# A two-layer decoder trunk: sums of the feed-forward layer on another engine, its second norm a quad later, and the last norm laid out as columns

## The chip, the cores and the metric

One core of a Trainium2 chip runs the kernel. The metric is the device time of one execution in microseconds; the kernel is run several times and the median is given, and one execution is recorded by the hardware profiler. TensorE (PE) multiplies matrices, VectorE (DVE) and ScalarE (ACT) work on tiles of 128 partitions, GpSimd (POOL) does so too, and SyncE (SP) issues most of the DMAs. PSUM holds what TensorE accumulates, SBUF everything else.

## The reference

Only the parts that the change touches are shown in full.

```python
def rmsnorm(x, g):
    xf = x.astype(jnp.float32)
    y = xf * lax.rsqrt(jnp.mean(xf * xf, axis=-1, keepdims=True) + EPS)
    return (y * g.astype(jnp.float32)).astype(x.dtype)

def swiglu(h, w_in, w_out):
    a = h @ w_in
    gate, up = jnp.split(a, 2, axis=-1)
    return (jax.nn.silu(gate) * up) @ w_out

def reference(x, mem, mix_norm, ...):
    for i in range(DEPTH):                       # DEPTH = 2
        h = rmsnorm(x, mix_norm[i])
        ...                                      # layer 0: HGRN2, layer 1: gMLP; and memory attention
        x = x + heads @ w_out[i]
        x = x + swiglu(rmsnorm(x, ffn_norm[i]), w_ffn_in[i], w_ffn_out[i])
    return rmsnorm(x, final_norm)
```

`x` is 1 x 1024 x 1024 (tokens by features), the feed-forward layer has 2816 hidden features, everything is float32.

## The kernel before

Activations lie with the features on the partitions: a tile is 128 features by 512 tokens, a "half" of the sequence, and `xn[half][kb]` is the residual stream, 8 tiles to a half. Every float32 product is made of three matmuls of a reduced type: an operand is cast to a high part (`hi` or `wh`, a cast on ScalarE, L150 and L130), the rest is the low part (`lo` or `wl`, a subtraction on VectorE, L152 and L132), and L457 (in the feed-forward layer; L157 to L159 and L684 elsewhere) multiplies hi by hi, hi by lo and lo by hi.

`ffn_in` takes the first product of the feed-forward layer in "quads": a quad is a 2 x 2 block of weight tiles against a 2 x 2 block of activations, done with seven products, named "1" to "7", in place of eight. So sums and differences of weights and of activations have to be made first. Three quads are opened early, while the output projection still runs, and the first two (`early`) go through all seven products side by side. The order is: `head1` (product "1") of the three quads, `head2` (product "2"), then products 3, 5, 6, 7 and 4 of the early two. `ready_b` makes the operands of the coming product out of the normed activations of the second half, which need `r`, the second norm's factor: `rest.rstd()` issues its matmul (L210) and then the chain in `rsqrt` (L223 adds eps, L227 and L228 are Ln and Exp, L229 to L231 one Newton step). It is called after the `head1` of quad 0. Ahead of product "6", `early_sums` makes the four weight sums of quad 2 on VectorE (L433 to L436; the third one is the weight of product "6"), and `ready_b("4")` makes the four tiles `t4` on VectorE (L541). L505 adds product "7" of an early quad.

`ffn_out` adds the second product to the residual. In layer 1 its last product ("4", from `CUT` = 4 on) runs in two slices of 256 tokens of the second half; L692 adds a block to the residual, `Sum.add` squares it on ScalarE (L196), and at the end of a slice `rstd` sums over the features: L210 multiplies by a matrix of ones, here in five passes, one for `acc` and one for each of the four newest squares. `final` then scales eight tiles on VectorE (L1178) and SyncE sends them out (L1179).

The tile framework orders each engine's instructions by a schedule of its own, and puts semaphore waits where a tile depends on another; an engine works strictly in its order.

## Time and profile before

| | us |
|---|---|
| median of three runs (lowest, highest) | 2127.53 (2127.23, 2128.64) |
| the profiled execution, its own time | 2128.59 |
| span of its trace | 2126.9 |
| TensorE busy (share) | 2097.6 (99%) |
| VectorE busy (share) | 1376.7 (65%) |
| ScalarE busy (share) | 902.5 (42%) |
| GpSimd busy (share) | 90.5 (4%) |

The span is the time from the first to the last event of the trace; 1.7 us of the execution lie around it. Busy time of TensorE counts matmuls of either clock level alike, so the granted clock has to be read beside it. An instruction's duration in the timeline is longer than the distance to the next one of its engine where the two overlap: matmuls of 128x512 are shown with 0.39 us and follow each other every 0.2265 us (three in 0.68 us). A row "x4" groups four instructions in a row. The value in brackets is the engine's idle time before the instruction and what ended it.

### The profile page before, as it was taken

The page shows a single profiled execution, that of the slowest core. Times are in us where ns is not written, and L with a number is a line of the kernel's source. Part 1 is how long each engine was busy: PE and PEld are TensorE (multiplying, and loading weights), DVE is VectorE, ACT ScalarE, POOL GpSimd, SP SyncE. Part 2 cuts the span into 40 slices and gives each one's busy share as a digit, 9 for nine tenths or more (in the row PEclk, how much of TensorE's full clock was granted, in tenths as well). Part 3 has the DMA queues.
Part 4 walks back from the last instruction along what each step waited for, and adds up shares of the span by engine and source line. Part 5 has one row for each costly group of instructions (what it writes and reads, how often), then busy time and mean ns, then how long its engine had stood idle before and what let it go on. Part 6 is the DMA issues. An engine that isn't in the chain of part 4 may idle for free.

```text
span 2126.9 us, 29399 instructions
## 1 busy us (share of the span) xinstructions
PE 2097.6 (99%) x11414; PEld 1739.3 (82%) x11414; DVE 1376.7 (65%) x2357; ACT 902.5 (42%) x1639; POOL 90.5 (4%) x90
## 2 busy tenths in 40 slices
PE   8999999999999999999999999999999999999998
PEld 7978788788778888888888997787788888888887
DVE  8685665763974655548986744547854554569884
ACT  6444442442543333334454534734433333343462
POOL 1100000001100000000001000011000000000012
PEclk9999999999999999999999999999999999999999
DMA  5400101132022221228454221131122221266442
GB/s 190 121 29 21 31 12 50 31 106 73 20 73 87 85 94 60 90 89 269 152 183 140 95 70 31 45 111 44 40 90 89 84 94 60 87 210 218 132 131 85
DMA packets 84811, 197.84 MB, mean 93 GB/s; under 512 B 9536, under 2 KB 11712, under 8 KB 84672
## 3 DMA queue, kind: packets, MB, share of 16 engines
q1 hardware_dynamic: 84672, 195.97, 28.1%
q8 instruction: 89, 1.46, 0.3%
q14 instruction: 50, 0.41, 0.1%
HBM read 163.95 MB, written 31.98 MB: 92 GB/s over the span
## 4 chain that ended last, share of the span: by engine, by line
PE 88%; DVE 5%; issue 1%; ACT 1%; DVEq 0%; ACTq 0%
PE mm L457 27%; PE mm L684 11%; PE sm L457 10%; PE sm L684 8%; PE mm L157 8%; PE mm L158 8%; PE mm L159 8%; PE sm L945 2%; DVE lo L152 1%; PE sm L357 1%; PE sm L346 1%; PE sm L1025 1%; PE sm L210 1%; PE sm L1006 1%; PE sm L1012 1%
## 5 line engine op out<-in xcount | busy, mean ns | idle before, releaser
L130 ACT CAST wh<-raw 128x512 fp32r<-128x512 f32 x454 | 271.0, 620 | 303.2 <-PE mm L158 106.4
L132 DVE TENSOR_TENSOR wl<-raw,wh 128x512 fp32r<-128x512 f32 x454 | 308.4, 693 | 101.4 <-ACT wh L130 91.8
L457 PE MATMUL mm<-hi,wh 128*128 128x512 f32 x832 | 324.5, 391 | 3.6 <-ACT wh L130 1.8
L457 PE MATMUL mm<-lo,wh 128*128 128x512 f32 x832 | 323.8, 391 | 0.0
L457 PE MATMUL mm<-hi,wl 128*128 128x512 f32 x832 | 323.3, 390 | 0.0
L157 PE MATMUL mm<-hi,wh 128*128 128x512 f32 x640 | 255.3, 399 | 6.2 <-ACT wh L130 6.1
L159 PE MATMUL mm<-hi,wl 128*128 128x512 f32 x640 | 253.4, 396 | 0.0
L158 PE MATMUL mm<-lo,wh 128*128 128x512 f32 x640 | 252.0, 394 | 0.0
L457 PEld LDWEIGHTS mm<-hi,wh 128*128 128x128 f32 x832 | 157.0, 189 | 37.8 <-ACT wh L130 2.7
L457 PEld LDWEIGHTS mm<-hi,wl 128*128 128x128 f32 x832 | 156.9, 189 | 32.8
L457 PEld LDWEIGHTS mm<-lo,wh 128*128 128x128 f32 x832 | 156.9, 189 | 32.7
L505 DVE TENSOR_TENSOR c<-mm,c 128x512 f32<-128x512 f32 x44 | 30.4, 690 | 191.5 <-PE mm L457 188.6
L157 PEld LDWEIGHTS mm<-hi,wh 128*128 128x128 f32 x640 | 120.8, 189 | 34.7 <-ACT wh L130 6.9
L159 PEld LDWEIGHTS mm<-hi,wl 128*128 128x128 f32 x640 | 120.7, 189 | 27.2 <-issue 2.1
L158 PEld LDWEIGHTS mm<-lo,wh 128*128 128x128 f32 x640 | 120.7, 189 | 27.1 <-issue 2.1
L684 PE MATMUL mm<-hi,wh 128*128 128x512 f32 (+1 forms) x380 | 142.9, 376 | 0.0
L684 PE MATMUL mm<-hi,wl 128*128 128x512 f32 (+1 forms) x380 | 141.9, 373 | 0.0
L684 PE MATMUL mm<-lo,wh 128*128 128x512 f32 (+1 forms) x380 | 141.9, 373 | 0.0
L457 PE MATMUL sm<-lo,wh 128*128 128x512 f32 x352 | 136.6, 389 | 0.0
L457 PE MATMUL sm<-hi,wl 128*128 128x512 f32 x352 | 136.6, 389 | 0.0
L457 PE MATMUL sm<-hi,wh 128*128 128x512 f32 x352 | 136.3, 389 | 0.0
L204 POOL TENSOR_TENSOR acc<-acc,sq 128x512 f32<-128x512 f32 x38 | 56.1, 1475 | 1616.6 <-ACT sq L196 1615.7
(263 smaller groups left out, 3955.8 us busy)
## 6 DMA issues: line engine op xcount, KB each, us to landing
raw<-in_wu_dram SPq DMA_DIRECT2D x168, 512.0 KB, 4.1
raw<-in_wu_dram SPq DMA_DIRECT2D x114, 256.0 KB, 3.5
hd<-c SPq DMA_DIRECT2D x88, 256.0 KB, 3.0
hid<-hd SPq DMA_DIRECT2D x88, 256.0 KB, 4.5
s<-in_wu_dram SPq DMA_DIRECT2D x22, 256.0 KB, 4.5
xin<-in_xT_dram SPq DMA_DIRECT2D x16, 256.0 KB, 5.6
xn<-in_xT_dram SPq DMA_DIRECT2D x16, 256.0 KB, 4.9
xs<-xn SPq DMA_DIRECT2D x16, 256.0 KB, 4.6
```

The lines of the kernel that those rows point to most:

```text
L130: nc.scalar.copy(hi, src)
L132: nc.vector.tensor_tensor(lo, src, hi.bitcast(F32), op=ALU.subtract)
L152: nc.vector.tensor_tensor(lo, src, hi.bitcast(F32), op=ALU.subtract)
L157: nc.tensor.matmul(ps, ah, bh, start=first, stop=False)
L158: nc.tensor.matmul(ps, ah, bl, start=False, stop=False)
L159: nc.tensor.matmul(ps, al, bh, start=False, stop=last)
L204: (nc.vector if self.count > 5 else self.adder).tensor_tensor(self.acc, self.acc, sq, op=ALU.add)
L210: nc.tensor.matmul(ps, ones_d, x, start=i == 0, stop=i == len(parts) - 1)
L457: nc.tensor.matmul(ps, a, b, start=start and i == 0 and k == 0, stop=i == 3 and k == 2, skip_group_check=True)
L505: nc.vector.tensor_tensor(self.p, self.b, self.p, op=ALU.add)
L684: nc.tensor.matmul(banks[d][:, sl], a, b, start=start and f == 0 and k == 0, stop=f == FH - 1 and k == 2, skip_group_check=True,)
L945: nc.tensor.matmul(o, keys, qd[:, queries].rearrange("p (b u n) -> p b u n", u=2, n=n)[:, :, 1, :], start=True, stop=True,)
```

## The change

There are four edits.

- In `rsqrt` the addition of eps on VectorE moves behind Ln and Exp in the code (everywhere the function is used). Ln takes eps as its own bias, so both read the same sums.
- In `ffn_in`, in both layers, the four `t4` differences and the four `early_sums` of quad 2 are made by GpSimd in place of VectorE, and `rest.rstd()` comes after the `head1` of quad 1.
- In the last slices (layer 1), three of the four newest squares are added to `acc` on VectorE, so that the matrix of ones is multiplied by two tiles in place of five. For the last slice the new `rstd_last` makes the means as columns (squares as the weights, one column of ones moving), takes the root of 128x2 numbers, spreads them and brings them back into rows with four transposes, twice, into two banks of PSUM; the tables of ScalarE aren't loaded again. Gains of three output tiles (`GAINED`) are multiplied in ahead of time.
- `final` lets GpSimd scale those three tiles and VectorE the other five, and the last slice's eight transfers go out from SyncE and ScalarE in turn.

```diff
+        def rstd_last(self):
+            nt = self.n // P
+            parts = [self.acc] + self.tails
+            ps = sm_ps()[:, :nt]
+            for t in range(nt):
+                for i, x in enumerate(parts):
+                    nc.tensor.matmul(
+                        ps[:, t : t + 1], x[:, t * P : (t + 1) * P], ones_d[:, 0:1],
+                        start=i == 0, stop=i == len(parts) - 1,
+                    )
+            r = rsqrt(ps, None, nt)
+            rb = nrm.tile([P, HALF], F32, name="rb", tag="n")[:, : self.n]
+            nc.vector.tensor_copy(
+                rb.rearrange("p (t f) -> p t f", f=P), r.unsqueeze(2).broadcast_to([P, nt, P])
+            )
+            res = []
+            for _ in range(2):
+                ps = sm_ps()[:, : self.n]
+                for t in range(nt):
+                    nc.tensor.transpose(ps[:, t * P : (t + 1) * P], rb[:, t * P : (t + 1) * P], ident)
+                res.append(ps)
+            return res
...
-            r = Sum(self.adder, sl.stop - sl.start, self.reload)
+            r = Sum(nc.vector, sl.stop - sl.start, self.reload)
...
-        nc.vector.tensor_scalar(a, ps, EPS, None, op0=ALU.add)
         if after is not None:
             with tc.issue_after(after.ins):
                 load_log_tables()
         nc.scalar.activation(r, ps, AF.Ln, bias=eps)
         nc.scalar.activation(r, r, AF.Exp, scale=-0.5)
+        nc.vector.tensor_scalar(a, ps, EPS, None, op0=ALU.add)
...
-        def early_sums(self):
+        def early_sums(self, eng=nc.vector):
-            nc.vector.tensor_tensor(a["22"], a["21"], a["22"], op=ALU.add)
+            eng.tensor_tensor(a["22"], a["21"], a["22"], op=ALU.add)
...
-                    nc.vector.tensor_tensor(d, first[4 + i][0], first[i][0], op=ALU.subtract)
+                    nc.gpsimd.tensor_tensor(d, first[4 + i][0], first[i][0], op=ALU.subtract)
...
             q.head1(t)
-            if i == 0:
+            if i == 1:
                 r = rest.rstd()
...
-                    q.early_sums()
+                    q.early_sums(nc.gpsimd)
...
-        sums = [Sum(), Sum()]
+        sums = [Sum(), Sum(reload=layer == 0)]
...
-                            add("4", d, total, sl, True)
-                        for _ in done(1, total.rstd(), sl):
+                            add("4", d, total, sl, d == 3)
+                        for _ in done(1, total.rstd_last() if sl.start else [total.rstd()] * 2, sl):
...
+            rv, rs = r
+            if sl.start:
+                rs = nrm.tile([P, HALF], F32, name="rs", tag="n")[:, : sl.stop - sl.start]
+                nc.scalar.copy(rs, r[1])
+            for n, d in enumerate((3, 0, 4, 5, 1, 6, 7, 2)):
+                o = xn[half][d][:, sl]
+                if d < GAINED:
+                    nc.gpsimd.tensor_tensor(o, o, rs, op=ALU.mult)
                 else:
+                    nc.vector.scalar_tensor_tensor(o, o, gain(C_FIN + d), rv, op0=ALU.mult, op1=ALU.mult)
+                (nc.scalar if sl.start and n % 2 else nc.sync).dma_start(out=out[d, half, :, sl], in_=o)
```

In the changed kernel the lines have other numbers: L152 is L153, L433 to L436 are L458 to L461, L457 is L482, L500 is L525, L505 is L530, L535 is L560, L541 is L566, L550 and L554 are L575 and L579, L130 is L131.

First place, layer 0, end of the early quads, on VectorE. `raw<-raw` at L433 to L436 are the weight sums, `t` at L541 the four differences, `c` are partial results of products. Before:

```order
L152 TENSOR_TENSOR lo<-hfb,hi 128x512
L434 TENSOR_TENSOR raw<-raw 128x512
L152 TENSOR_TENSOR lo<-hfb,hi 128x512
L435 TENSOR_TENSOR raw<-raw 128x512
L500 TENSOR_TENSOR c_5717<-sm,c_5717 128x512
L436 TENSOR_TENSOR raw<-raw 128x512
L500 TENSOR_TENSOR c_5732<-sm,c_5732 128x512
L541 TENSOR_TENSOR t_5735<-hfa 128x512
L541 TENSOR_TENSOR t_5737<-hfa 128x512
L541 TENSOR_TENSOR t_5739<-hfa 128x512
L541 TENSOR_TENSOR t_5741<-hfa 128x512
L152 TENSOR_TENSOR lo<-t_5735,hi 128x512
```

And GpSimd after the change, in the same place:

```order
L566 TENSOR_TENSOR t_5735<-hfa 128x512
L566 TENSOR_TENSOR t_5737<-hfa 128x512
L458 TENSOR_TENSOR raw<-raw 128x512
L566 TENSOR_TENSOR t_5739<-hfa 128x512
L459 TENSOR_TENSOR raw<-raw 128x512
L566 TENSOR_TENSOR t_5741<-hfa 128x512
L460 TENSOR_TENSOR raw<-raw 128x512
L461 TENSOR_TENSOR raw<-raw 128x512
```

The eight stand in one row on GpSimd, the two kinds in turn; on VectorE they are gone, and the low parts of `t` follow those of `hfb` with only two L525 and one L579 between.

Second place, the same stretch on ScalarE. `wh_5822` is the cast weight of product "6" of quad 2, made of the third weight sum; `hi_5743` to `hi_5755` are the casts of the four `t4`. Before:

```order
L130 CAST wh_5822<-raw_5099 128x512
L130 CAST wh_5826<-raw_5695 128x512
L550 ACTIVATE c12_5717<-c12_5717 128x512
L130 CAST wh_5830<-raw_5695 128x512
L130 CAST wh_5834<-raw_5099 128x512
L150 CAST hi_5743<-t4_5735 128x512
```

After:

```order
L575 ACTIVATE c12_5717<-c12_5717 128x512
L131 CAST wh_5822<-raw_5099 128x512
L151 CAST hi_5743<-t4_5735 128x512
L131 CAST wh_5826<-raw_5695 128x512
L151 CAST hi_5747<-t4_5737 128x512
L131 CAST wh_5830<-raw_5695 128x512
L151 CAST hi_5751<-t4_5739 128x512
```

The cast of the weight now stands directly ahead of the cast of the first `t4`, and the other weight casts stand between those of `t4`. On TensorE two matmuls of product "6" of quad 2 stand ahead of the first of product "4" of quad 0 in both kernels.

Third place, the end of the program, on ScalarE. `xn_12713` and `xn_12900` are the output tiles 0 and 2, which GpSimd scales first and last after the change; `xn_13035` and `xn_13066` are tiles 5 and 6. Before:

```order
L196 ACTIVATE sq_18383<-xn_13066 128x256
L196 ACTIVATE sq_18407<-xn_13097 128x256
L179 ACT_TABLE_LOAD
L227 ACTIVATE r_18415<-sm_18409,eps_84 128x256
L228 ACTIVATE r_18415<-r_18415 128x256
```

After:

```order
L197 ACTIVATE sq_18412<-xn_13097 128x256
L251 ACTIVATE r_18419<-sm_18414,eps_84 128x2
L252 ACTIVATE r_18419<-r_18419 128x2
L1213 COPY rs_18435<-sm_18432 128x256
L1221 DMA out_0_dram<-xn_12713 128x256
L1221 DMA out_0_dram<-xn_12900 128x256
L1221 DMA out_0_dram<-xn_13035 128x256
L1221 DMA out_0_dram<-xn_13066 128x256
```

Behind the root, now on two columns, ScalarE copies the scales and issues four of the eight transfers, that of tile 2 second.

## Rows read from the trace of the kernel before

**Rows 1.** The page, section 1: busy time of TensorE and the others.

```profile
PE 2097.6 (99%) x11414; PEld 1739.3 (82%) x11414; DVE 1376.7 (65%) x2357; ACT 902.5 (42%) x1639; POOL 90.5 (4%) x90
```

**Rows 2.** TensorE's waits: engine, line, releaser, us in total, times, longest.

```profile
PE sm L210 <- DVE acc L204: 3.1, 2, 1.6
PE mm L457 <- ACT wh L130: 1.8, 2, 0.9
PE mm L457 <- DVE c L505: 1.8, 2, 0.9
...
PE mm L157 <- DVE qm L814: 0.9, 1, 0.9
```

**Rows 3.** Timeline: start us, us, engine, line, [idle before]; layer 0's second norm.

```profile
558.36 1.13 PE L210 MATMUL sm<-acc,ones_d 128*128 128x512 f32 x2 [1.54 <-DVE acc L204]
...
560.24 0.69 ACT L227 ACTIVATE r<-sm,eps 128x512 f32<-128x512 f32 x1 [0.77 <-DVE a L223]
```

**Rows 4.** Timeline, TensorE, end of layer 0's early quads.

```profile
594.85 0.39 PE L457 MATMUL mm<-hi,wh 128*128 128x512 f32 x1
...
596.83 0.50 PE L457 MATMUL mm<-hi,wh 128*128 128x512 f32 x1 [0.92 <-ACT wh L130]
...
598.46 0.50 PE L457 MATMUL mm<-hi,wh 128*128 128x512 f32 x1 [0.90 <-DVE c L505]
...
603.13 0.39 PE L457 MATMUL mm<-hi,wh 128*128 128x512 f32 x1
```

**Rows 5.** Timeline, VectorE and ScalarE in the same stretch.

```profile
586.29 1.88 DVE L535 TENSOR_TENSOR hfb<-hfb 128x512 f32<-128x512 f32 x3
...
593.03 1.14 ACT L130 CAST wh<-raw 128x512 fp32r<-128x512 f32 x2 [2.28 <-DVE raw L435]
...
594.72 2.48 DVE L541 TENSOR_TENSOR t<-hfa 128x512 f32<-128x512 f32 x4
```

**Rows 6.** Windows: stretch, its length, busy us of each engine, granted clock, DMA.

```profile
595.00:605.00 10.00, 8.18 (x29) 5.93 (x28) 9.42 (x16) 5.08 (x10) 0.00 (x0) 0.83 0.20 79
```

**Rows 7.** Timeline: GpSimd's sums alone, and beside VectorE's.

```profile
478.40 1.28 POOL L204 TENSOR_TENSOR acc<-acc,sq 128x512 f32<-128x512 f32 x1 [69.71 <-ACT sq L196]
...
511.58 1.67 DVE L434 TENSOR_TENSOR r<-raw,r 128x512 f32<-128x512 f32 x1
...
2026.86 4.88 POOL L204 TENSOR_TENSOR acc<-acc,sq 128x512 f32<-128x512 f32 x3 [556.84 <-ACT sq L196]
...
2027.09 1.79 DVE L152 TENSOR_TENSOR lo<-hid,hi 128x512 fp32r<-128x512 f32 x1
...
2028.80 1.78 DVE L613 TENSOR_TENSOR raw<-raw 128x512 f32<-128x512 f32 x1
```

**Rows 8.** Timeline: the tail, after the last product.

```profile
2114.73 0.28 PE L684 MATMUL mm<-hi,wl 128*128 128x256 f32 x1
...
2115.28 1.89 PE L210 MATMUL sm<-sq,ones_d 128*128 128x256 f32 x8
...
2115.57 0.42 ACT L196 ACTIVATE sq<-xn 128x256 f32<-128x256 f32 x1 [2.16 <-DVE xn L692]
...
2116.00 1.28 ACT L179 ACT_TABLE_LOAD   x1
...
2120.08 3.26 DVE L1178 SCALAR_TENSOR_TENSOR xn<-xn,gn,r 128x256 f32<-128x256 f32 x8
...
2120.59 3.80 SPq L1179 DMA_DIRECT2D out_dram<-xn  x8
```

**Rows 9.** Groups by shape: count, busy us, mean ns, idle before.

```profile
L346 PE MATMUL sm<-ident,pr 128*128 128x128 f32 x128 | 19.1, 278 | 0.3 <-DVE pr L338 0.3
...
L291 PE MATMUL sm<-ones_d,acc 128*128 128x1 f32 x16 | 1.9, 239 | 0.0
...
L229 DVE TENSOR_TENSOR a<-a,r 128x4 f32<-128x4 f32 x2 | 0.3, 153 | 0.0
...
L227 ACT ACTIVATE r<-sm,eps 128x4 f32<-128x4 f32 x2 | 0.5, 255 | 0.0
```

More of the change, by code (lines that the diff above doesn't have):

```diff
@@ L31 @@
 MAIN_AHEAD = 2
+GAINED = 3
 LN_EXP_SET = 6
@@ L427, in second @@
             self.a["21"], self.a["22"] = r2[:, :HALF], r2[:, HALF:]
-        def early_sums(self):
+        def early_sums(self, eng=nc.vector):
             a = self.a
             self.weights("4")
-            nc.vector.tensor_tensor(a["22"], a["21"], a["22"], op=ALU.add)
-            nc.vector.tensor_tensor(a["21"], a["11"], a["21"], op=ALU.subtract)
-            nc.vector.tensor_tensor(a["11"], a["22"], a["11"], op=ALU.subtract)
-            nc.vector.tensor_tensor(a["12"], a["12"], a["11"], op=ALU.subtract)
+            eng.tensor_tensor(a["22"], a["21"], a["22"], op=ALU.add)
+            eng.tensor_tensor(a["21"], a["11"], a["21"], op=ALU.subtract)
+            eng.tensor_tensor(a["11"], a["22"], a["11"], op=ALU.subtract)
+            eng.tensor_tensor(a["12"], a["12"], a["11"], op=ALU.subtract)
             a["5"], a["7"], a["6"], a["3"] = a["22"], a["21"], a["11"], a["12"]
@@ L715, in ffn_out @@
                 banks = x_banks if p in "1674" else y_banks
+            if layer == 1 and p == "4" and f == CUT:
+                for d in range(GAINED):
+                    x = xn[1][d]
+                    nc.scalar.activation(x, x, AF.Copy, scale=gain(C_FIN + d))
             if layer == 1 and p == "4" and f >= CUT:
@@ L1171, in final @@
         def final(half, r, sl):
-            for d in range(KB):
-                o = xn[half][d][:, sl]
-                if half == 0:
+            if half == 0:
+                for d in range(KB):
+                    o = xn[half][d][:, sl]
                     nc.scalar.activation(o, o, AF.Copy, scale=gain(C_FIN + d))
                     nc.gpsimd.tensor_tensor(o, o, r, op=ALU.mult)
-                else:
-                    nc.vector.scalar_tensor_tensor(o, o, gain(C_FIN + d), r, op0=ALU.mult, op1=ALU.mult)
-                nc.sync.dma_start(out=out[d, half, :, sl], in_=o)
-                yield
+                    nc.sync.dma_start(out=out[d, half, :, sl], in_=o)
+                    yield
+                return
+            rv, rs = r
[3 more added lines that the diff above has]
+            for n, d in enumerate((3, 0, 4, 5, 1, 6, 7, 2)):
+                o = xn[half][d][:, sl]
+                if d < GAINED:
+                    nc.gpsimd.tensor_tensor(o, o, rs, op=ALU.mult)
+                else:
+                    nc.vector.scalar_tensor_tensor(o, o, gain(C_FIN + d), rv, op0=ALU.mult, op1=ALU.mult)
+                (nc.scalar if sl.start and n % 2 else nc.sync).dma_start(out=out[d, half, :, sl], in_=o)
+            yield
         ffn_out(1, ex, xn, hd[1], final)
```

## The prediction

> **What bounds the kernel now.** I began with the page: TensorE is busy 99% of the span and VectorE 65% [rows 1]. So only places where TensorE idles or runs at half clock can be won, and only places where a moved step makes it idle can be lost. The table of TensorE's waits names those that this change touches [rows 2]: 3.1 us for the matmul of the second norm's mean squares (L210, twice, once per layer), 1.8 and 1.8 us at L457 for a weight cast on ScalarE and for a sum on VectorE (each twice), and 0.9 us for `qm`. I then read the timeline around them in layer 0. Layer 1 repeats it 921.6 us later, so every price of a layer counts twice.
>
> At 558.36 the norm's matmul has kept TensorE idle for 1.54 us [rows 3]. At the end of the early quads TensorE is at the first matmul of product "6" of quad 2 at 594.85; then come the two waits of 0.92 and 0.90, and a stretch with a granted clock of 0.83, which is half clock (1.2 GHz) for part of it [rows 4, 6]. The row at 603.13 stands 19 matmuls behind the one at 594.85; at the 0.2265 us of full pace it would be at 599.15. So this place costs 4.0 us, and with the norm a layer loses **5.5 us**. VectorE is busy 9.42 of those 10 us [rows 6]: it feeds TensorE just too late, which is what the moved sums are about. The tail is a chain in which TensorE has no part left: from the end of the last product at 2115.01 to the end of the span at 2126.88 go 11.87 us [rows 8].
>
> **The change, step by step.**
>
> *Second norm one quad later.* A full head of matmuls now stands between the last square sum and L210, more than the 1.54 us of the wait [rows 3]: **-1.54 us per layer**. L210 comes at about 559.5, 1.2 us later than now. Part comes back at once: Ln waited 0.77 us for the eps addition that read the same bank [rows 3], and that addition now stands behind Exp. The norm `r` is therefore ready about 0.5 us later than now, and VectorE's chain of normed operands with it.
>
> *Eight sums per layer from VectorE to GpSimd.* VectorE saves 8 issues of 0.60 us (the four of L541 take 2.48 us, 0.60 from one to the next [rows 5]), 4.8 us. What GpSimd needs: alone, a 128x512 addition takes 1.28 us [rows 7]. Beside VectorE it is another story: three in a row take 4.88 us, and VectorE's additions with both inputs in SBUF take 1.79, 1.78 and 1.67 us there, where one of them takes 0.68 (the four of L541: 2.48 less three steps of 0.60) [rows 5, 7]. The two engines alternate: one VectorE addition and one GpSimd addition per 1.71 us (2027.09 to 2028.80). A sum that collides thus costs VectorE 1.1 us where it saved 0.60; if all 8 collide, VectorE has 8 x 1.1 - 4.8 = 4.0 us more to do, in a stretch where it has nothing to spare.
>
> The Trainium skill says why such a thing can be ("SBUF — State Buffer", Who interferes with whom): a VectorE instruction with two SBUF inputs contends with a GpSimd instruction that reads SBUF, because its second input comes through the shared interface. The trace agrees with 1.79 against 0.68 us. The same list says that an instruction with at most one SBUF input does not contend; no row quoted here shows that side, and if most of VectorE's work here were of that kind the rival without collisions below would be the outcome.
>
> What TensorE waits for: GpSimd's order is t4[0], t4[1], L458, t4[2], L459, t4[3], L460, L461. The third weight sum (now L460) makes the weights "6" of quad 2, and their cast on ScalarE is followed at once by the two matmuls that now stand at 594.85. Before, that sum ended on VectorE in time for the cast at 593.03 [rows 5]. Now the first t4 waits for a buffer that VectorE's second L535 releases; that one ends at 586.97 [rows 5], with the later norm at about 587.4. Seven sums at 1.71 us end at **599.4**, the cast (half of the 1.14 us of two, plus its start) at **600.0**. TensorE, with 1.54 us won, would be at this place at 593.3: it loses **6.7 us** up to there. ScalarE has the casts of t4 queued behind that weight cast, and VectorE its low parts behind those casts and between the colliding additions. By the same alternation I place the 24 following matmuls 1.4 us over their pace. Half clock goes on top: now 10 us at 0.83, 1.7 us [rows 6]; under waits that last anyway it costs less, I take 1.0. Sum 9.1 us against 5.5 before: **+3.6 us per layer, +7.2 in all**. Bounds: without any collision the seven sums take 9.0 us, the cast is there at 597.1, TensorE loses 3.8 us plus 1.7 of half clock, 5.5, so nothing changes; with half clock after the wait as long as before, and the low parts late by one more alternation of 1.71, it is 9.1 + 0.7 + 0.6 or more, +5.
>
> *Last slices.* Three of five partial sums are now added on VectorE between the products, so the first slice's ten matmul passes of L210 become four. Eight passes take 1.89 us, 0.216 from one to the next [rows 8]; six fewer are **-1.30 us**, and the last product ends at 2113.7. Behind it, old chain: 11.87 us. New chain, by the nearest rows: the addition and its square as before (1.0 us, the square ends at 2115.99); no table load (1.28 us before, which ran beside L210's passes [rows 8]); four 128x1 matmuls, 0.24 each, overlapped (0.6); Ln and Exp and four small VectorE steps at 0.25 and 0.15 each, with 0.05 between (1.4) [rows 9]; a 128x256 copy (0.5 with its start, from the 0.41 of a product); four transposes of 0.28 (0.6) [rows 9]: scales ready after 4.1 to 4.3. Five VectorE products of 0.41 [rows 8] end at 6.4. The longer arm is GpSimd's: its copy of the scales on ScalarE (5.3), three 128x256 products at half of 1.28 (7.3), and then ScalarE's queue, which issues d0, d2, d5, d6 in this order and so holds d5 and d6 until GpSimd's last product; three issues 0.50 apart (the eight of SP take 3.80 us) and the 2.5 us from the last issue to the end that SP's show [rows 8] make 10.8. No row shows an issue on ScalarE; at the pace of SP as I take it, and with d5 and d6 free, 10.0, or 11.0 if GpSimd's products collide. **-1.1 there, -2.4 with the first slice** (-3.2 to -1.5).
>
> *The rest.* The eps addition behind Exp also shortens the other norms' chains, and `qm` now follows `r` directly on VectorE, which can end the 0.9 us wait [rows 2]. Elsewhere the order moves both ways: **-0.9** (-2 to +1).
>
> Net: 7.2 - 2.4 - 0.9 = **+3.9 us**. The profiled execution took 2128.59 us, 1.06 above the median of three; on it the sum gives 2132.5, on the median 2127.53 it gives **2131.4**. A measurement of this kernel can tell about 0.2%, 4.25 us, so the borders are 2123.3 and 2131.8; the forecast lies just inside "no change", leaning to slower.
>
> **The rivals.** *GpSimd's chain costs more than the sum has (slower).* Where the low parts of t4 are the last to come, VectorE's split of each meets GpSimd's L461 and the gating work, and TensorE falls to half clock after the 6.7 us wait, as it does now after the waits of 0.9. +5.5 per layer, about 2135. It decides from the point at which more than two of the operand splits behind L460 are late. For it: VectorE is busy 9.42 of 10 us there now, and each wait of 0.9 was followed by half clock. Against it: the slow stretch is partly spent waiting anyway.
>
> *No collisions, but a late chain (no change to slightly faster).* GpSimd at 1.28, VectorE unhindered: 0 per layer, only tail and rest are left, 2127.53 - 3.3 = 2124.2. For it: many VectorE steps in the stretch read PSUM or one tensor. Against it: three rows out of three in which the two engines meet show 1.67 to 1.79.
>
> *The sums are hidden, as the edit says (faster).* VectorE's freed 4.8 us bring its operands early, the weights "6" come in time, the 4.0 us and the 1.54 us go: -11.0 - 3.3, 2113; with half of that left in the way, 2118. The Trainium skill leaves this open ("Perfetto Trace Analysis", Optimizing Scalar/DVE Operations): when VectorE is saturated, moving work to other engines may make sense, though between VectorE and GpSimd it might not help. The row for GpSimd speaks against it: even at 1.28 seven sums take 9.0 us from 587, and TensorE wants the result at 593.
>
> **How the numbers follow.** Forecast 0.48, centred on 2131.4 and reaching from 2129 to 2134, so that 0.18 of it lies over 2131.8; the slower rival 0.20; the case without collisions 0.18, of which 0.04 below 2123.3; the hidden sums 0.14. Faster 0.18, same 0.44, slower 0.38. The range leaves out the hidden sums and the upper tail of the slower rival: 2122.5 to 2136.5.
>
> **What would show it.** Right: in TensorE's waits L210 (now L211) is gone and a wait of several us for the cast of weights (now L131) or for GpSimd's L460 stands at L482, twice; GpSimd's additions there 1.6 us or more, VectorE's beside them 1.7; the granted clock again below 1 in the ten us behind; the last product 1.3 us earlier against the end of the first slice, the chain behind it near 10.8 us, with ScalarE's queue issuing last. Wrong: GpSimd's sums at 1.28 us beside VectorE's at 0.68, or L460 done before TensorE comes to its product. It would also fall if the planner's new order elsewhere moved more than 2 us either way.

## The result

| | median us (lowest to highest) |
|---|---|
| before, with the runs beside the changed kernel | 2128.09 (2127.23 to 2129.43) |
| changed kernel | 2140.17 (2139.61 to 2142.11) |
| ratio, 95% interval | 1.006 (1.0048 to 1.0073) |

The changed kernel is 12 us slower, 10 to 16 by the interval. The forecast said 2131.4 and its range ended at 2136.5. The profiled execution of the changed kernel took 2142.11 us with a span of 2140.3; all traces below are set against the profiled execution of before (2128.59, span 2126.9), 13.5 us apart. The changed kernel's profiled execution was the slowest of its four, 1.9 us over their median.

On the page of the changed kernel, section 1, TensorE is busy 98% ([rows 1]: 99%) and GpSimd 126.4 us in place of 90.5:

```profile
PE 2103.5 (98%) x11410; PEld 1739.9 (81%) x11410; DVE 1372.1 (64%) x2342; ACT 904.4 (42%) x1642; POOL 126.4 (6%) x112
```

The table of TensorE's waits (us in total, times, longest) answers to [rows 2]. L482 was L457, L131 was L130, L530 was L505:

```profile
PE mm L482 <- ACT wh L131: 10.9, 2, 5.5
...
PE mm L158 <- DVE qm L844: 2.1, 2, 1.8
...
PE sm L234 <- DVE rb L227: 1.7, 1, 1.7
PE mm L482 <- DVE c L530: 1.6, 2, 0.8
...
PE mm L482 <- DVE c L499: 1.0, 2, 0.5
...
PE sm L221 <- ACT sq L197: 0.9, 1, 0.9
PE mm L710 <- DVE c L579: 0.5, 1, 0.5
```

The wait of the second norm's matmul (L210, now L211) is gone as forecast. The wait for a weight cast at L482 went from 1.8 to 10.9 us, 5.5 in each layer. `qm`, which was to vanish, went from 0.9 to 2.1. New are waits for `c` at L499, for `rb` and for the square in the tail (L234, L221), and for a gating product (L579) at the start of `ffn_out`.

The windows of the same kernel (stretch, its length, busy us of PE, PEld, DVE, ACT, POOL, granted clock, DMA share, GB/s), of layer 0 and layer 1, answer to [rows 6]:

```profile
595.00:605.00 10.00, 4.30 (x14) 2.37 (x13) 3.95 (x5) 2.08 (x4) 9.16 (x7) 0.92 0.07 26
605.00:615.00 10.00, 9.40 (x32) 7.60 (x33) 7.91 (x14) 4.35 (x9) 0.00 (x0) 0.74 0.33 106
1520.00:1530.00 10.00, 5.75 (x23) 3.69 (x21) 5.74 (x7) 1.94 (x4) 10.00 (x7) 0.92 0.07 26
1530.00:1540.00 10.00, 7.99 (x21) 5.94 (x22) 7.34 (x12) 6.31 (x12) 1.79 (x2) 0.57 0.20 61
```

TensorE is busy 4.30 of the 10 us from 595, and the granted clock is below 1 for two windows, down to 0.57 in layer 1; before it was one window of 0.83. VectorE is busy only 3.95 us from 595: it is no longer the engine that is late, it waits too.

Where the 13.4 us of the span come from can be read by setting the n-th matmul of the two traces side by side. Ahead of layer 0's feed-forward layer (matmul 4000) the changed kernel is 3.4 us behind, after the early quads (4400) 8.6, early in `ffn_out` (6000) 9.4, after layer 1's early quads (8800) 15.0; the tail gives 1.6 back. So the early quads cost 5.2 and 5.6 us, the rest ahead of them 3.4, the start of `ffn_out` 0.8. A time in layer 0's early quads has therefore to be read less 3.34 us (matmul 4100, just ahead of them, starts at 549.85 before and at 553.19 after the change) before it is set against a time of the kernel before, one in layer 1's less 9.4.

The timeline shows the early quads of layer 0. First GpSimd's first `t4`, VectorE's rows beside the sums and after its pause, then GpSimd's following sums, ScalarE's casts and TensorE:

```profile
590.22 3.95 POOL L566 TENSOR_TENSOR t<-hfa 128x512 f32<-128x512 f32 x1 [38.34 <-ACT hi L151]
...
592.93 0.68 DVE L525 TENSOR_TENSOR c<-sm,c 128x512 f32<-128x512 f32 x1
593.53 1.20 DVE L153 TENSOR_TENSOR lo<-hfb,hi 128x512 fp32r<-128x512 f32 x1
...
596.34 1.77 DVE L579 TENSOR_TENSOR c<-c,c 128x512 f32<-128x512 f32 x1
604.16 0.69 DVE L153 TENSOR_TENSOR lo<-t,hi 128x512 fp32r<-128x512 f32 x1 [6.05 <-ACT hi L151]
...
595.83 1.73 POOL L458 TENSOR_TENSOR raw<-raw 128x512 f32<-128x512 f32 x1
597.52 1.71 POOL L566 TENSOR_TENSOR t<-hfa 128x512 f32<-128x512 f32 x1
599.19 1.26 POOL L459 TENSOR_TENSOR raw<-raw 128x512 f32<-128x512 f32 x1
...
601.63 1.26 POOL L460 TENSOR_TENSOR raw<-raw 128x512 f32<-128x512 f32 x1
...
602.92 0.62 ACT L131 CAST wh<-raw 128x512 fp32r<-128x512 f32 x1 [8.64 <-POOL raw L460]
603.45 0.61 ACT L151 CAST hi<-t 128x512 fp32r<-128x512 f32 x1
...
603.59 0.79 PE L482 MATMUL mm<-hi,wh 128*128 128x512 f32 x1 [5.48 <-ACT wh L131]
...
606.16 0.63 PE L482 MATMUL mm<-lo,wh 128*128 128x512 f32 x1
606.59 0.63 PE L482 MATMUL mm<-hi,wl 128*128 128x512 f32 x1
```

The first `t4` starts at 590.22 and takes 3.95 us; before, a sum on GpSimd took 1.28 alone and 1.6 beside VectorE [rows 7]. The third weight sum, L460, starts at 601.63. ScalarE has been idle for 8.64 us when the cast of that sum begins, and behind it stand the casts of `t4`, the first of which had been ready since 594. TensorE gets its operand at 603.59, and then runs at half clock: its matmuls follow each other 0.43 us apart, in place of 0.2265, until 610. VectorE loses 0.5 to 1.1 us at each of three instructions beside GpSimd's sums (593.53, 595.25 and 596.34), 2.1 us in all, and then stands for 6.05 us until ScalarE has cast the first `t4`. So in this kernel the collisions cost time through GpSimd's own chain, and not through VectorE.

### The profile page after: what moved, and what is told of

Same layout as the page of the kernel before. It is cut to its first block, busy times and chain, and to the rows that moved or that the text cites. A ratio compares the mean times of both kernels' runs of the same rounds, so it can differ in the third digit from the quotient of the medians.

```text
span 2140.3 us, 29433 instructions
## 1 busy us (share of the span) xinstructions
PE 2103.5 (98%) x11410; PEld 1739.9 (81%) x11410; DVE 1372.1 (64%) x2342; ACT 904.4 (42%) x1642; POOL 126.4 (6%) x112
## 4 chain that ended last, share of the span: by engine, by line
PE 89%; DVE 3%; issue 1%; POOL 1%; ACT 1%; POOLq 0%; DVEq 0%; ACTq 0%
PE mm L482 27%; PE mm L710 11%; PE sm L482 10%; PE mm L158 9%; PE mm L160 8%; PE mm L159 8%; PE sm L710 8%; PE sm L975 2%; PE sm L382 1%; PE sm L371 1%; PE sm L1055 1%; DVE lo L153 1%; PE sm L1041 1%; PE sm L1036 1%; PE sm L1042 1%
## 5 line engine op out<-in xcount | busy, mean ns | idle before, releaser
L131 ACT CAST wh<-raw 128x512 fp32r<-128x512 f32 x454 | 271.4, 620 | 321.5 <-PE mm L159 109.0
L482 PE MATMUL mm<-hi,wh 128*128 128x512 f32 x832 | 325.6, 393 | 12.5 <-ACT wh L131 10.9
L482 PE MATMUL mm<-lo,wh 128*128 128x512 f32 x832 | 325.8, 392 | 0.1
L482 PE MATMUL mm<-hi,wl 128*128 128x512 f32 x832 | 324.3, 391 | 0.0
L482 PEld LDWEIGHTS mm<-hi,wh 128*128 128x128 f32 x832 | 157.7, 190 | 47.9 <-ACT wh L131 11.8
L482 PEld LDWEIGHTS mm<-lo,wh 128*128 128x128 f32 x832 | 157.6, 189 | 34.0 <-DVE lo L153 1.6
L482 PEld LDWEIGHTS mm<-hi,wl 128*128 128x128 f32 x832 | 157.2, 189 | 32.9
L530 DVE TENSOR_TENSOR c<-mm,c 128x512 f32<-128x512 f32 x44 | 30.4, 690 | 194.7 <-PE mm L482 194.6
L482 PE MATMUL sm<-hi,wl 128*128 128x512 f32 x352 | 137.0, 389 | 0.0
L482 PE MATMUL sm<-lo,wh 128*128 128x512 f32 x352 | 136.8, 390 | 0.0
L482 PE MATMUL sm<-hi,wh 128*128 128x512 f32 x352 | 136.5, 390 | 0.0
```

The costliest lines, as they stand in the source:

```text
L131: nc.scalar.copy(hi, src)
L482: nc.tensor.matmul(ps, a, b, start=start and i == 0 and k == 0, stop=i == 3 and k == 2, skip_group_check=True)
L530: nc.vector.tensor_tensor(self.p, self.b, self.p, op=ALU.add)
```

## The experiments

The theories, by the names that the expectations use: **A**, the late chain (GpSimd's sums end late, ScalarE's casts queue behind them, TensorE stands still); **B**, the collisions (VectorE loses time beside GpSimd); **S**, the eps order costs in the start. Medians of before beside these runs lay between 2127.1 and 2127.6.

**All sums back on VectorE.**

```diff
-                    nc.gpsimd.tensor_tensor(d, first[4 + i][0], first[i][0], op=ALU.subtract)
+                    nc.vector.tensor_tensor(d, first[4 + i][0], first[i][0], op=ALU.subtract)
...
-                    q.early_sums(nc.gpsimd)
+                    q.early_sums()
```

> The changed kernel with the eight sums of each layer back on VectorE; everything else of the change stays (norm a quad later, eps addition behind Exp, new tail). Theory A (the late chain: TensorE stands still because the GpSimd sums end late and ScalarE's casts queue behind them) and theory B (the collisions: VectorE loses time beside GpSimd) agree here: the wait of 5.5 us for the weight cast goes, per layer the sums' +6.2 and +6.6 us come back, about 2127.4 (2126 to 2129). A third view, that the norm or the eps addition costs in the feed-forward layers, expects more than 2132.

2128.27 us, ratio 1.0003 (0.9994 to 1.0012). What both theories expected came true. The eight sums carry the loss, 11.9 us; all other edits together come to 1.1 us on the medians, with zero inside the interval.

**The sums alone, on the kernel before** (both edits above, the other way).

> The kernel before with one edit: the eight sums of each layer on GpSimd, the norm where it was. Theory A+B (GpSimd is starved until VectorE reads PSUM, then both alternate, ScalarE's casts queue behind the late weight sum): +5 to +6.5 us per layer as in the changed kernel, 2137 to 2140. If the damage hung on the later norm (which moved the sums into a fuller stretch of VectorE): +2 per layer, 2131.

2138.93 us, ratio 1.0057 (1.004 to 1.0074). The sums cost the same without the other edits, so the later norm is not what made them expensive. In this kernel GpSimd's order is another (a weight sum first, then the two kinds in turn), and TensorE's long wait of 5.4 us is ended by VectorE's L505 in layer 0 and by a cast of `t4` in layer 1. The rows of layer 0 lead back to the same place:

```profile
597.55 0.62 ACT L130 CAST wh<-raw 128x512 fp32r<-128x512 f32 x1 [6.18 <-POOL raw L435]
...
601.26 0.76 PE L457 MATMUL mm<-hi,wh 128*128 128x512 f32 x1 [5.41 <-DVE c L505]
```

ScalarE stands until GpSimd has made the third weight sum; the first cast of `t4` comes behind that cast, its low part on VectorE behind it, and L505 behind the low part.

**Eight more sums that nobody waits for.**

```diff
+                scr = ntile("scr")
+                nc.gpsimd.tensor_tensor(scr, t["b12"][1], t["b12"][1], op=ALU.subtract)
+                for _ in range(7):
+                    nc.gpsimd.tensor_tensor(scr, scr, scr, op=ALU.subtract)
                 t["7"] = [split(t["b12"][i], ex, "e") for i in range(4)]
```

> The kernel before with eight additional GpSimd subtractions per layer at the place of the sums, into a spare tile that nothing reads; VectorE keeps all its own sums. So the collisions are there, and nobody waits for GpSimd. Theory B: 8 x 1.1 us of VectorE time per layer in a stretch where it is full, +6 to +9 us per layer, 2140 to 2146. Theory A: VectorE loses a part of that in the shadow of other waits and the starved GpSimd takes its turn mostly when VectorE pauses, at most +1.5 us per layer, 2128 to 2131.

2137.91 us, ratio 1.005 (1.0035 to 1.0065): collisions alone cost 10.8 us here. Theory A's expectation was missed, and theory B's (2140 to 2146) by 2 us. VectorE still has its own eight sums in this kernel, 4.8 us per layer more than in the changed one, so 10.8 is not the collisions' share there. The timeline of this kernel, GpSimd and VectorE in layer 0:

```profile
587.64 6.78 POOL L537 TENSOR_TENSOR scr<-hfb 128x512 f32<-128x512 f32 x1 [38.70 <-DVE hfb L535]
594.50 5.71 POOL L539 TENSOR_TENSOR scr<-scr 128x512 f32<-128x512 f32 x4
...
593.43 0.69 DVE L500 TENSOR_TENSOR c<-sm,c 128x512 f32<-128x512 f32 x1
...
595.49 5.26 DVE L545 TENSOR_TENSOR t<-hfa 128x512 f32<-128x512 f32 x4
```

The four differences of L545 (L541 of before) take 5.26 us in place of 2.48 [rows 5], 1.45 from one to the next. And the first extra sum takes 6.78 us: beside nine of VectorE's instructions with two SBUF inputs, 0.60 us apart, it doesn't get through, and it ends 0.99 us after VectorE began L500, which reads PSUM. TensorE's waits:

```profile
PE mm L457 <- DVE c L505: 8.9, 2, 4.4
...
PE mm L457 <- ACT wh L130: 2.5, 2, 1.3
```

**The same place, without GpSimd's reads.** A first run had eight memsets in place of the eight subtractions.

> As the run with the eight extra GpSimd subtractions, but they are eight memsets of the same 128x512 tile: GpSimd is as busy at the same place and reads nothing from SBUF. If the loss of the extra sums comes from GpSimd's reads beside VectorE's instructions with two SBUF inputs: no starving, VectorE at 0.68 us, and the time of the kernel before, 2126 to 2128.5. If it comes from GpSimd being busy there at all, or from the spare buffer and the waits for it: 2134 to 2138 as with the subtractions.

2127.20 us, ratio 0.9998 (0.9988 to 1.0007). But the memsets were executed 14 us earlier, since nothing bound them to the place. A second run kept the first subtraction, which binds the rest:

```diff
+                scr = ntile("scr")
+                nc.gpsimd.tensor_tensor(scr, t["b12"][1], t["b12"][1], op=ALU.subtract)
+                for _ in range(16):
+                    nc.gpsimd.memset(scr, 0.0)
```

> As the run with eight extra GpSimd subtractions: the first is the same subtraction, which binds the rest to the same place; the other seven are replaced by sixteen memsets of the tile (0.53 us each, 8.4 us, as long as seven subtractions). If GpSimd's reads are the cause: VectorE takes 0.68 us beside them, TensorE's waits are those of the kernel before, 2126.5 to 2129. If being busy, the buffer or the wait for it are the cause: 2134 to 2138.

2128.28 us, ratio 1.0003 (0.9993 to 1.0013). Its timeline:

```profile
586.88 6.78 POOL L537 TENSOR_TENSOR scr<-hfb 128x512 f32<-128x512 f32 x1 [38.71 <-DVE hfb L535]
593.71 9.28 POOL L539 MEMSET scr<- 128x512 f32 x16
...
594.72 2.48 DVE L545 TENSOR_TENSOR t<-hfa 128x512 f32<-128x512 f32 x4
```

GpSimd is busy for 9.28 us in the same stretch and VectorE's four differences take 2.48 us beside it, as before, and the time is what was expected of that cause. It is GpSimd's reads of SBUF that hold VectorE up, not its being busy, nor the spare tile. The one subtraction that reads is starved for 6.78 us here too.

**Only the weight sums on GpSimd.**

> The changed kernel with the four differences t4 back on VectorE; the four weight sums of quad 2 stay on GpSimd. Theory A: GpSimd starts with the low part of weights 4 at about 592.4, three sums at 1.3 to 1.7 end at 596.5 to 597.5, TensorE wants the cast at about 593.5 to 595: a wait of 1.5 to 3 us in place of 5.5, with one slot of half clock; 2131 to 2135. Theory B: half the sums, half the loss over x1, +3.2 per layer, 2133.8.

2129.88 us, ratio 1.0014 (1.0004 to 1.0023), below both expectations: 1.6 us over the run with all sums on VectorE. GpSimd's timeline:

```profile
590.77 1.63 POOL L458 TENSOR_TENSOR raw<-raw 128x512 f32<-128x512 f32 x1 [40.69 <-DVE wl L133]
...
594.18 1.61 POOL L460 TENSOR_TENSOR raw<-raw 128x512 f32<-128x512 f32 x1
```

No sum is starved here: the first one is released 0.4 us before VectorE begins L525, which reads PSUM, and ends 1.25 us after that. Without `t4` ahead of it the third weight sum ends at 595.8, and the waits for weight casts (2.7 us for both layers) are what they are with all sums on VectorE (2.6).

**Only `t4` on GpSimd.**

> The changed kernel with the four weight sums back on VectorE; the four differences t4 stay on GpSimd. Theory A+B: the first t4 is starved until VectorE reads PSUM (about 594), the casts of t4 on ScalarE stand ahead of weight casts, TensorE waits 3 to 5 us per layer; 2133 to 2138, more than the run with only the weight sums (2129.9), since t4 starts later and its casts hold up the weight casts. If the weight sum's cast were the whole of the loss: 2128 to 2129.

2125.60 us, ratio 0.999 (0.9981 to 1.0): the expectation was wrong by more than 7 us, and the other view (2128 to 2129) by 2.4. The first difference is starved longer than in the changed kernel, and it doesn't matter, since on GpSimd nothing that is wanted earlier stands behind it:

```profile
588.60 6.96 POOL L566 TENSOR_TENSOR t<-hfa 128x512 f32<-128x512 f32 x1 [38.38 <-ACT hi L151]
...
594.33 0.68 DVE L525 TENSOR_TENSOR c<-sm,c 128x512 f32<-128x512 f32 x1
```

It starts at 588.60 and ends at 595.56, 1.23 us after the start of VectorE's L525 at 594.33, that is, the time of one undisturbed sum (1.26 to 1.28). In the changed kernel the first `t4` ended at 594.17, 1.24 us after L525 at 592.93.

So neither kind costs much by itself: against the run with all sums on VectorE the weight sums on GpSimd add 1.6 us on the medians, the differences take 2.7 away, and both together add 11.9. By the trace of the changed kernel, what costs is that the two kinds share one queue, in which the third weight sum stands behind the four differences.

**The weight sums earlier**, first without `t4` on GpSimd, then with it.

```diff
-            if name == "6":
+            if name == "5":
                 for q in quads[2:]:
```

> As the run with only the weight sums on GpSimd, but quad 2's second half is loaded and summed one product earlier (ahead of product 5). The number of sums beside VectorE is the same. Theory A: the chain is done before TensorE comes to it, the wait for that cast goes, and VectorE has 2.4 us less to do: 2124 to 2128. Theory B: the same loss as in the run with the weight sums at their old place, 2131 to 2134.

2130.66 us, ratio 1.0013 (1.0004 to 1.0023), between both expectations. The wait for that weight cast went, and a wait of 2.5 us per layer for a cast of normed activations came, 27 us earlier, where the sums now meet VectorE's norm chain: its three steps behind Exp take 1.58 to 1.66 us each in place of 0.69. Nothing was won by moving the place.

> The changed kernel, all eight sums on GpSimd, but quad 2's sums are issued one product earlier, so that on GpSimd the four weight sums stand ahead of the four differences. Order theory: the weight cast of product 6 no longer waits for a starved t4, the 5.5 us waits go; with the 2.5 us wait that the earlier place brought at 572 us it is 2128 to 2132. Number theory (eight sums cost what they cost, in any order): 2137 to 2141.

2135.22 us, ratio 1.0032 (1.0021 to 1.0044), between both expectations. TensorE's waits in this kernel:

```profile
PE sm L482 <- ACT hi L151: 4.8, 2, 2.5
PE mm L482 <- DVE lo L153: 3.6, 4, 1.6
```

The wait for the weight cast is gone: with the weight sums made ahead of the differences, the 5.5 us go. This run makes the third one much earlier as well as ahead (at 564.75 in place of 601.63), so by itself it can't tell order from time; the run with only the weight sums on GpSimd, at their old place and with no wait for a weight cast over 1.4 us, speaks for the order. What is left is the 2.4 per layer of the earlier place and 1.5 for a low part of `hfb`, an operand of product "7". That low part is late by collisions, for here the first difference was not starved:

```profile
593.10 1.58 POOL L566 TENSOR_TENSOR t<-hfa 128x512 f32<-128x512 f32 x1 [25.04 <-DVE hfb L560]
...
593.45 1.78 DVE L560 TENSOR_TENSOR hfb<-hfb 128x512 f32<-128x512 f32 x1
```

It got through at once, between two instructions with two SBUF inputs each, and held VectorE's second up by 1.1 us; the low part behind took 1.75 us in place of 0.69.

**The norm a quad later, alone.**

> The kernel before with one edit: the second norm is taken after the first head of quad 1. If the 1.54 us wait at L210 goes and its chain is not late elsewhere: -1.5 us per layer, 2124. If VectorE's operands come 0.5 to 1.2 us later and the waits at the end of the early quads grow by what was won: 2126 to 2128.

2129.04 us, ratio 1.0006 (0.9997 to 1.0016), over both expectations. The 1.54 us wait [rows 3] is gone and nothing is won. TensorE's rows with waits in layer 0:

```profile
566.16 0.50 PE L457 MATMUL sm<-hi,wh 128*128 128x512 f32 x1 [0.36 <-ACT hi L150]
...
597.11 0.50 PE L457 MATMUL mm<-hi,wh 128*128 128x512 f32 x1 [1.57 <-ACT wh L130]
```

A wait of 0.36 is new, the wait for the weight cast grew from 0.92 to 1.57 [rows 4]; counted by matmuls, the kernel is 1.9 us ahead of the one before behind L210 (matmul 4150), 0.7 ahead at 586 us (4250), where the waits for sums haven't begun, and 0.3 us per layer behind at the end of the early quads.

**The eps addition behind Ln and Exp, alone.**

> The kernel before with one edit: the eps addition stands behind Ln and Exp. Theory S (the new order of ScalarE and VectorE at the start costs more than the shorter chains give): the wait for qm at 59 us becomes 1.8 us in place of the 0.8 for v, small waits behind it, +2 us before the feed-forward layer, 2128 to 2130. The forecast's view: -0.9 us, about 2126.

2128.88 us, ratio 1.0007 (0.9998 to 1.0017): in the direction of theory S, though a zero is not excluded. Its waits:

```profile
PE mm L157 <- DVE qm L814: 2.1, 2, 1.9
PE sm L210 <- DVE acc L204: 2.1, 2, 1.0
```

At 58.78 TensorE stands for 1.86 us for `qm`, where the kernel before stood 0.8 for `v`, and the granted clock of the ten us from 60 is 0.85 in this trace. In the feed-forward layers the wait at L210 falls from 3.1 to 2.1 us for both.

**Norm and tail without sums and eps order** (the eps addition late in the last two slices only).

> The changed kernel with the eight sums back on VectorE and the eps addition back ahead of Ln, except in the two last slices. If sums and eps order carry all of the loss, the norm's 1 to 1.5 us per layer and the tail's 1.6 to 2.3 us are left as a gain: 2122 to 2123.5. If not, 2127 or more.

2126.71 us, ratio 1.0001 (0.9992 to 1.001): neither expectation, and 1.9 us more than the tail alone (next run). Its trace gets 1.8 us back in the tail but is 2.4 us later than the kernel before when the tail begins, so the tail's gain is there and the norm's isn't.

**The tail alone, and with other queues.**

> The kernel before with the new tail alone (squares added on VectorE between the products, last norm as columns, GpSimd's three tiles, two queues; eps addition behind Exp in the two last slices only). Forecast's term: -2.4 us, of which -1.3 from the first slice; the traces with all edits say -1.6 to -2.3: 2125 to 2125.5.

2124.86 us, ratio 0.9989 (0.998 to 0.9999): -2.5 on the medians, the forecast's -2.4.

```diff
-            for n, d in enumerate((3, 0, 4, 5, 1, 6, 7, 2)):
+            for d in (3, 4, 5, 0, 6, 7, 1, 2):
...
-                (nc.scalar if sl.start and n % 2 else nc.sync).dma_start(out=out[d, half, :, sl], in_=o)
+                (nc.scalar if sl.start and d in (4, 6, 7) else nc.sync).dma_start(out=out[d, half, :, sl], in_=o)
```

> As the run with the new tail alone, but the last slice's transfers of tiles 4, 6 and 7 go out from ScalarE and the other five from SyncE, so that no tile of VectorE stands behind GpSimd's third on ScalarE. If that queue's order holds the end (last issue at GpSimd's third product plus two more issues), the end comes 0.5 to 1 us earlier than with the tail alone: 2124 to 2125. If not, the same time as the tail alone.

2124.93 us, ratio 0.9985 (0.9975 to 0.9994), no different from the tail alone. The order of ScalarE's queue did hold the end in the changed kernel, as the rows of its last us show:

```profile
2133.70 2.65 SPq L1221 DMA_DIRECT2D out_dram<-xn  x4
2134.06 2.09 POOL L1218 TENSOR_TENSOR xn<-xn,rs 128x256 f32<-128x256 f32 x3 [9.51 <-ACT rs L1213]
2134.82 2.72 ACTq L1221 DMA_DIRECT2D out_dram<-xn  x4
```

GpSimd's third product ends at 2136.15 and ScalarE issues until 2137.54, 1.2 us longer than SyncE. With the other queues they read:

```profile
2116.48 2.77 SPq L1224 DMA_DIRECT2D out_dram<-xn  x5
2116.65 2.09 POOL L1221 TENSOR_TENSOR xn<-xn,rs 128x256 f32<-128x256 f32 x3 [9.09 <-ACT rs L1216]
2116.88 1.63 ACTq L1224 DMA_DIRECT2D out_dram<-xn  x3
```

ScalarE issues until 2118.51, SyncE until 2119.25, and the last issue ends 0.5 us behind GpSimd's third product in place of 1.4. In the traces the chain behind the last product is 9.99 us in place of 10.63 with the tail alone; a gain of 0.6 us is below what the medians can tell.

**What is worth keeping: `t4` and the tail.** With the norm later, and then with the norm where it was:

> Of the change: the four differences t4 on GpSimd, the norm a quad later, the new tail with tiles 4, 6 and 7 going out from ScalarE; weight sums on VectorE, eps addition ahead of Ln except in the last slices. VectorE has four sums less in the stretch that took the norm's gain back: if that backlog was the reason, the norm now gives its 1.5 us per layer, 2121 to 2123.5. If not, the tail's gain alone, 2124.5 to 2126.

2123.72 us, ratio 0.9982 (0.9972 to 0.9991), between both expectations.

> As the run before it, with the norm back at its old place (after the first head of quad 0). If the norm counts once t4 is gone from VectorE, this one is 2 to 3 us slower than that run; if t4 on GpSimd is what helped and the norm gives nothing, both are equal.

2122.91 us, ratio 0.9977 (0.9967 to 0.9987): 4.6 us faster than before, 17 than the changed kernel, and the fastest of all. The later norm gives nothing here either, though VectorE has four sums less to do: 0.8 us lie between the two runs, to the earlier norm's credit, and the intervals overlap. TensorE's waits at the early quads of both layers, and the windows around them:

```profile
PE mm L485 <- DVE c L533: 0.8, 2, 0.4
...
PE mm L485 <- ACT wh L131: 0.8, 2, 0.4
```

```profile
595.00:605.00 10.00, 8.98 (x35) 6.27 (x36) 9.55 (x15) 6.09 (x12) 4.24 (x3) 1.00 0.20 79
1515.00:1525.00 10.00, 8.93 (x35) 6.10 (x35) 9.55 (x15) 6.26 (x12) 4.42 (x3) 1.00 0.21 80
```

Each wait of 0.9 [rows 2] is down to 0.4, and in this profiled execution the granted clock stays at 1.00 in both layers ([rows 6]: 0.83).

## Why the prediction was wrong

The sign of the lean was right, as was the mechanism of the sums; the size was not: the net of +3.9 us was 12.1 on the medians and 13.5 in the profiled execution. Of the 9.5 us by which the span missed the sum, 3.6 lie in the early quads, 5.1 in the term "the rest" and 0.8 in the tail. On the medians the sums come to 11.9 against 7.2, and all other edits, with the sums on VectorE, to +1.1 against the -3.3 of tail and rest. So two steps failed: the price of the half clock inside the sums, and the gain of the rest.

*The sums.* Forecast, with the norm: +3.6 us per layer; measured 5.2 and 5.6. The wait for the third weight sum's cast came, behind GpSimd's chain in the order that was read from the program, with ScalarE's casts of `t4` behind it. Read less the 3.34 us by which the changed kernel entered the layer late, layer 0 sets against the forecast as follows.

| | forecast | measured (times less 3.34) |
|---|---|---|
| GpSimd's chain of seven sums begins | 587.4 | 586.9 |
| it ends | 599.4 | 599.55 |
| the cast is done | 600.0 | 600.2 |
| first matmul of product "6" of quad 2 behind the one of before | 5.15 us | 5.4 us (layer 1: 5.4) |
| the 19 matmuls from there, over full pace | 1.4 + 1.0 us | 3.8 us (layer 1: 4.2) |

The chain and what waits for it were right, in part by luck: the first sum took 3.95 us where 1.71 was taken, and the last three 1.26, because VectorE had run out of work. The step that failed here is the half clock. It was priced at 1.0 us, with the reason that it costs less under waits that last anyway. But the clock was low behind the wait and not under it: 13 matmuls from 603.59 on (14 in layer 1) went at about 0.43 us apart, which is 3.0 us over full pace in layer 0 and 3.3 in layer 1. The late low parts, priced at 1.4, came to one wait of 0.79. Alone a sum takes 1.28 us, so by this estimate meeting VectorE made the chain 3.7 us longer (12.67 us in place of 7 x 1.28).

The working had also assumed that the two engines alternate from the start. In the changed kernel they did only once GpSimd had got its first turn. [rows 7] shows a meeting in which GpSimd was served at once, and so does the run with the weight sums first; what decides between the two cases is not shown.

The sentence of the Trainium skill ("SBUF — State Buffer", Who interferes with whom), that VectorE with two SBUF inputs contends with a GpSimd instruction that reads SBUF, was borne out: VectorE's four differences take 5.26 us beside GpSimd's subtractions and 2.48 beside its memsets. So was the other side that the prediction left open: VectorE's L525, with one input in PSUM, takes 0.68 us beside GpSimd's sums (592.93). The Trainium skill's rule in the same section that issue order decides who blocks is near to what the starved sum shows, but the blocked engine waited here for more than one instruction, up to 6.96 us in all.

*The rivals.* The slower rival had +5.5 us per layer, from half clock after the long wait and late low parts. Its half clock came, its price for a layer was right, and it stood at 2135 only because it too counted 3.3 us of gains for tail and rest. The sums "hidden, as the edit says" failed for the reason given there: the result was wanted at 598.1 (TensorE was held up before, too) and came at 602.9. Half of that edit was good, though. With `t4` alone on GpSimd the median falls by 2.0 us (2122.91 against 2124.93, with tail and queues alike), by 2.7 against the run with all sums on VectorE and by 3.0 with norm and tail; only in the last pair do the intervals lie apart, and there the queues differ too. Where both traces have the full clock, the early quads of layer 0 are just 0.1 us shorter by matmuls, and the start of `ffn_out` 0.7. That the shorter waits keep the clock up in more executions would account for the rest; it isn't shown. The forecast had priced the eight sums as one chain and so could not see this.

*The norm.* Counted at -1.54 us per layer, with 0.5 us of lateness for VectorE's operands beside it. The run with that edit alone gives nothing, and all three pairs of runs with and without it lean to slower (1.9 us alone, 1.9 with the tail, 0.8 with tail and `t4`). TensorE comes earlier to operands that are not earlier: 1.2 of the 1.9 us won are lost again by 586 us, ahead of the sums. VectorE is busy for 37.33 of the 38 us from 566 to 604, and the idle time at L210 was only the first place where its pace showed. In the changed kernel 0.2 us of the 1.54 were left when TensorE came to the cast. The 1.54 should have been put against VectorE's chain and not against TensorE's wait. The backlog of the sums is not what takes it back, since with `t4` on GpSimd it gives nothing either.

*The rest.* In the traces this step of the sum failed by the most. Counted at -0.9, measured +3.4 before the first feed-forward layer and +0.8 at the start of `ffn_out`. The `qm` wait of 0.9 at 29 us fell to 0.2, as read from the order; the one at 59 us took its place with 1.84, and the granted clock fell behind it (0.83 in the ten us from 60). With the eps edit alone that clock loss shows as well; with all sums on VectorE the same wait of 1.84 passes at full clock, and that kernel enters the layer 2.0 us late. So about 1.4 of the 3.4 is the luck of the profiled execution, the other 2.0 the order. The prediction named this as a sign of being wrong: a new order elsewhere that moves more than 2 us.

*The tail.* -2.4 forecast, -2.5 measured alone, -1.6 in the changed kernel's trace. The chain behind the last product, 10.8 by the forecast, took 10.63 us alone and 11.35 in the changed kernel, and the late issue of ScalarE's queue came as worked out.

Part of the loss stays unassigned: the sums cost 11.8 alone and 11.9 in the changed kernel, all other edits together nothing that can be measured, but the split of the sums' part between collisions and order depends on the kernel. Collisions without a waiter cost 10.8, all of the sums with the weight sums first and earlier 7.7, `t4` alone less than nothing. These don't add, because in each case another engine is late next. The two traces set side by side matter too: the trace of before has half clock of its own in the early quads, while that of the run with all sums on VectorE has the full clock there, and against it the early quads of the changed kernel cost 7.2 and 7.5 us in place of 5.2 and 5.6.

## What to carry to other kernels

A wait that TensorE shows in a stretch where another engine is busy all the time is likely that engine's time: here the wait at L210 went and nothing was won. Before work goes to an engine whose reads collide with those of the full one, split it by when each result is wanted: in this kernel the differences, wanted last, were starved for 7 us at no cost, and the weight sum, wanted first, cost 5.5 us behind them in the same queue. Price a moved sum from rows in which the two engines really meet in the same pattern. And price the half clock behind a long wait by itself, from a row of matmuls at either pace; here it did not hide under the wait.

## What the runs showed of the hardware that was not expected

GpSimd's first sum beside an unbroken row of VectorE instructions with two SBUF inputs waited up to 5.7 us (6.96 against 1.26) and ended 1.23 us after VectorE began an instruction that reads PSUM, in two kernels to 0.01 us of each other. Once it had its turn, the two alternated at about 1.7 us a pair. Neither is a rule: in the run with the weight sums first a sum got through such a row at once (1.58 us, in both layers), and in the changed kernel an addition of squares at 544.95, which took 3.36 us, ended 1.23 us after VectorE began an instruction that reads no PSUM.

The granted clock after the same waits differed from one profiled execution to the next: with two waits of 0.9 in the early quads of layer 0 it was 0.83 over ten us before the change and 1.00 with the tail alone, and by matmuls that is 1.6 us per layer. Executions of one kernel lay up to 4.6 us apart, which is why edits worth 1 us were read here from traces as well as from medians.
